# Sparse attention in a two-layer trunk: heads in pairs at the products with the values, the compressed branch padded to 128 rows, output projections in three parts

## The chip, the cores and the metric

The kernel runs on one core of one Trainium2 chip. The metric is the device time of one execution in microseconds (us), lower is better. Every product is made in float32 accuracy by splitting each operand into a high and a low float32r part (named `hi` and `lo`, or `wh` and `wl` for weights) and adding three products: high by high, high by low and low by high.

## The reference, cut to what matters

The program is a decoder trunk of two layers over one sequence of 256 tokens with a model width of 2048. Layer 0 mixes tokens by native sparse attention (NSA) with 16 heads of 128 columns in 4 groups of 4; layer 1 mixes them by gated linear attention (GLA). After each mixer comes an MLP with 8192 hidden columns.

```
o_cmp = einsum(p_cmp, v_cmp)      # 15 compressed keys, padded to 16
o_sel = ...; o_win = ...          # at 256 tokens both are causal attention over all keys
o = gts[...,0:1]*o_cmp + gts[...,1:2]*o_sel + gts[...,2:3]*o_win
y = o.reshape(b, s, nh*d) @ w_out # 2048 x 2048
x = x + y;  x = x + squared_relu_mlp(rms_norm(x))
```

A group of 4 heads shares its keys and values. The gates are multiplied into the probabilities, so that all three branches of a head are summed in one accumulator.

## The kernel before, in words

**The plan.** The program text is written out by a planner, the class `Plan` (line 34). It keeps a clock for each engine; each helper adds its own estimated cost to the clock (`mm` on line 158, `transpose` on 167, `act`, `copy`, `tt`, `ts`). Side work is written as Python generators ("streams"), spawned with `W.spawn`. A stream yields the planned time at which it may go on (`W.ready`: the end of the work that made its inputs, plus `MARGIN` of 250 ns) and the buffers that it needs. `W.tick` is called after every few matmuls of the main work and lets each stream whose time has come emit its next instructions; it returns at once while ACT or DVE is planned to be more than `slack` (2500 ns) behind PE. `W.drain` runs one stream to its end at the place where the main work needs it, whether its inputs are ready on the chip or not. So the costs in `mm` and `transpose` decide where each side instruction lands in each engine's queue, in the whole program. `mode_b`, which the MLP uses for its first product, passes its own slack of 2500 or 5000 ns; `a_half`, which makes all projections, uses the default.

**Main work of the NSA layer.** `nsa` (973) makes ten projections of 512 columns: compressed keys, compressed values, then twice keys, values and the queries of two groups. Each is 16 row tiles x 2 token tiles x 3 products = 96 matmuls of 512 columns, by `mode_a` and `a_half`. Each half unit of weights (512 KB) is split into `wh` by ACT and `wl` by DVE, three half units ahead of use.

**A head.** `queries` (1281) transposes a group's queries, takes an `operand()` tile `oT` for the group's output and spawns `attend` (1305) for each head. `attend` makes scores and exponentials for the two token tiles into one of 3 tiles `p`, applies gates, transposes `p` in six 128x128 pieces, and the compressed probabilities `p3` (high, high and low part, 3 x 16 = 48 columns for each token tile) in two more. The transposes go to two `aux` banks (of 4) in PSUM; ACT copies them to `pT` and `pTc` and DVE makes the low part of `pT`. `pT` has one slot (980), so that a head's transposes are emitted after the products of the head before. Lines 1407 to 1423 make the products with the values: for four blocks of keys three matmuls each, over 256 or 128 tokens, and one with `vC` on 48 rows:

```
mm(dst, v[:, 0, t, gs], ph_, ...)       # n = 256 or 128 columns
mm(dst, v[:, 0, t, gs], pl_, ...)
mm(dst, v[:, 1, t, gs], ph_, ...)
mm(po[:, 0:T], vC[:, g, :], pTc, ...)   # 48 rows, 256 columns
```

**Compressed keys and values.** `compress` (1118) works in four steps with tiles of `qT`, `pT` and `op` slots; for the values it ends with four small products that give `vC` (lines 1248 to 1264). The heads of the first group wait for both compress streams.

**Output projection.** `out_proj` (608), used by NSA and GLA, takes the contraction (16 row tiles, 4 for each group) in two halves of 8 tiles; in each half come the four column blocks `b`, each with 48 matmuls. `add_block` (602) has DVE add the two accumulators to the residual `xt`. In the first block of a half, `ready` (1450) drains the query stream and the head that each tile needs. After the last half's block `b`, `after.start(b)` (732) spawns the next MLP's preparation of that block: 8 transposes on PE, 4 scaled copies on ACT, 4 low parts on DVE, then two squares on ACT. The MLP's first unit (`mode_b`, 584) uses row tiles 0 to 7 of two weight units and then tiles 8 to 15, and drains the preparation of each tile (`prep.before`, 661).

Of the kernel before, what the change touches and what calls it, by code (L numbers as in the profile page):

```python
# [10 lines left out]
F32 = mybir.dt.float32  # L11
# [7 lines left out]
P = 128  # L19
T = 256  # L20
# [13 lines left out]
class Plan:  # L34
# [62 lines left out]

    def tick(self, slack=2500.0):
        taken = set()
        for s in list(self.streams):  # L100
            if max(self.t["act"], self.t["dve"]) > self.t["pe"] + slack:
                return
            if s["ready"] <= self.t["pe"]:
                if not (taken & set(s["need"])) and self.can(s["need"]):
                    self._step(s)
                else:
                    taken |= {tag for tag, n in s["need"].items() if not self.can({tag: n})}
# [16 lines left out]
def trunk_kernel(ctx: ExitStack, tc: tile.TileContext, a: dict, out: bass.AP):  # L124
# [33 lines left out]
    def mm(dst, lhsT, rhs, **kw):  # L158
        n = free(rhs)
        if lhsT.dtype == F32R:  # L160
            c = n / 2.4 + 3 if n >= 128 else 107.0
        else:
            c = max(4 * n / 2.4 + 3, 214.0)
        W.run("pe", c, [dst], [lhsT, rhs])
        nc.tensor.matmul(dst, lhsT, rhs, skip_group_check=True, **kw)  # L165

    def transpose(dst, src, idn):
        W.run("pe", 56.0 if src.dtype == F32R else 110.0, [dst], [src])
        nc.tensor.transpose(dst, src, idn)  # L169
# [331 lines left out]
    for b in range(10):  # L501
        for kg in range(4):
            weights.both(a["nsa_in"][b, kg])
        if b == 3:
            weights.both(a["nsa_gate"], 48)

    def out_units(w):
        for half in range(2):
            for b in range(NB):
                for kg in range(2):  # L510
                    weights.both(w[b, 2 * half + kg])
    out_units(a["nsa_out"])


# [93 lines left out]
    def out_proj(oTs, after, ready):  # L608

        for half in range(2):  # L610
            for b in range(NB):
                ps = acc()
                mode_a(oTs, ps, list(range(8 * half, 8 * half + 8)), ready if b == 0 else None)
                add_block(ps, b)
                if half == 1:
                    after.start(b)
            for g in (2 * half, 2 * half + 1):
                W.give(oTs[g])
# [354 lines left out]
    def nsa(prep, after):  # L973
        op = prep.op
        G, HPG = 4, 4
        with tc.tile_pool(name="nsa1", bufs=1) as s1, tc.tile_pool(name="nsa2", bufs=1) as s2:
            t4 = slotted(s2, "t4", 2)
            qtile = slotted(s2, "qT", 5)
            ptile = slotted(s2, "p", 3)
# [4 lines left out]
            def tables():  # L984
# [21 lines left out]
                nc.sync.dma_start(stack, a["gate_stack"])  # L1006
                vsel = s1.tile([48, 16], F32, name="vsel")[:, 0:2]
                nc.sync.dma_start(vsel, a["cmp_sel"])
                cst.update(identr=identr, maskr=maskr, gcol=gcol, w2=w2, pe=pe, stack=stack, vsel=vsel)
                yield 50000.0  # L1010
                vcopy(maskr, maskf)
                ts(gcol[:, 0:1], gcol[:, 0:1], SCALE, None, ALU.mult)
                W.give(maskf, W.t["dve"])
# [29 lines left out]
            vv = [s1.tile([P, 2, NT, 512], F32R, name=f"vv{i}") for i in range(2)]  # L1043
            vC = s1.tile([48, G, P], F32R, name="vC")
            gt = s1.tile([P, NT, 48], F32, name="gt")
# [72 lines left out]
            def compress(ps, which):  # L1118
# [127 lines left out]
                else:  # L1246

                    ge3 = zpool.tile([P, G, 3, 16], F32, tag="sq", name="ge3", bufs=2)
                    vcopy(ge3, ge.rearrange("p (g c) -> p g c", c=16).unsqueeze(2).to_broadcast([P, G, 3, 16]))
                    yield W.ready(ge3), {"aux": 1, "p": 2}  # L1250
                    pv = aux([P, 512])
                    for g in range(G):
                        mm(pv[:48, g * P:(g + 1) * P], ge3[:, g, :, :].rearrange("p a c -> p (a c)"),
                           w2[:, 1, :], start=True, stop=True)
                    vh = ptile([48, 512], F32R)
                    copy(vh, pv[:48, :])
                    yield W.ready(vh)
                    vl = ptile([48, 512])
                    tt(vl, pv[:48, :], vh.bitcast(F32), ALU.subtract)
                    W.give(pv, W.t["dve"])  # L1260
                    ts(vl, vl, cst["vsel"][:, 1:2], None, ALU.mult)
                    stt(vC.rearrange("p g d -> p (g d)"), vh.bitcast(F32), cst["vsel"][:, 0:1], vl, ALU.mult, ALU.add)
                    W.give(vh, W.t["dve"])
# [17 lines left out]
            def queries(ps, g, heads, waits):  # L1281
                yield 0.0, {"t4": 1}
                qs = t4([P, NT, 512])
                yield from normed(qs, ps)
                yield 0.0, {"rope": 1}
                rope(qs, cst["tabs"][0])
                for w in waits:
                    while not w["done"]:
                        yield 0.0
                yield 0.0, {"op": 1}  # L1290
                oT = operand()
                oTs[g] = oT
                for hh in range(2):
                    yield W.ready(qs), {"aux": 1, "qT": 2}
                    pt = transposed(qs, [(2 * hh + j) * P for j in range(2)])
                    qTs = [qtile([P, 2, T], F32R) for _ in range(2)]
                    yield from evac_splits([(qTs[j][:, 0, :], qTs[j][:, 1, :],
                                             pt[:, j, :, :].rearrange("p t k -> p (t k)"), cst["gcol"][:, 0:1])
                                            for j in range(2)])
                    give(pt)  # L1300
                    for j in range(2):
                        heads.append(W.spawn(attend(g, 2 * hh + j, qTs[j], oT)))
                W.give(qs)

            def attend(g, h, qT, oT):
                k = kT[g]
# [69 lines left out]

                p3 = small.tile([P, NT, 3, 16], F32R, tag="p3", name=nm("p3"))
                copy(p3[:, :, 0:2, :], pc.unsqueeze(2).to_broadcast([P, NT, 2, 16]))
# [3 lines left out]
                tt(p3[:, :, 2, :], pc, p3[:, :, 0, :].bitcast(F32), ALU.subtract)  # L1382
                yield W.ready(p, p3), {"aux": 2, "pT": 1}

                pta = aux([P, 512])
                ptb = aux([P, 512])
                ptc = ptb[:, 256:512].bitcast(F32R)
# [9 lines left out]
                pT = pttile([P, 2, 768], F32R)  # L1397
                pTc = small.tile([48, T], F32R, tag="pTc", name=nm("pTc"), bufs=2)
# [4 lines left out]
                tt(pT[:, 1, 0:512], pta, pT[:, 0, 0:512].bitcast(F32), ALU.subtract)  # L1403
                W.give(pta, W.t["dve"])
                tt(pT[:, 1, 512:768], ptb[:, 0:256], pT[:, 0, 512:768].bitcast(F32), ALU.subtract)
# [12 lines left out]
                mm(po[:, 0:T], vC[:, g, :], pTc, start=False, stop=True)  # L1418
                W.give(pT)
                copy(oT[:, h, 0, :], po[:, 0:T])  # L1420
                yield W.ready(oT)
                tt(oT[:, h, 1, :], po[:, 0:T], oT[:, h, 0, :].bitcast(F32), ALU.subtract)
                W.give(po, W.t["dve"])
# [424 lines left out]
def _constants():  # L1848
# [28 lines left out]
    c["gate_stack"] = np.concatenate([np.eye(48), np.eye(48)], 0).astype(np.float32)  # L1877
    low = (np.arange(48) // 16 == 1).astype(np.float32)
    c["cmp_sel"] = np.stack([1.0 - low, low], 1)

# [85 lines left out]
```

## Time and profile before

| what | value |
|---|---|
| median of 3 runs | 2179.98 us (2179.89 to 2184.03) |
| the profiled execution, its own time | 2175.89 us |
| its span in the profile | 2174.1 us |
| PE (matmul) busy | 2162.6 us, 99% |
| DVE, ACT, POOL busy | 1742.7 us (80%), 1363.7 us (63%), 151.4 us (7%) |
| granted TensorE clock | 1.0 in every slice (its upper level, 2.4 GHz) |
| DMA | 483.81 MB, mean 223 GB/s |

The span runs from the first to the last instruction; some 1.8 us of the execution lie around it. A matmul's own duration in the trace overlaps with that of its neighbours, so what one costs is read from the distance between the starts of two neighbours.

### The profile page before, as it was taken

What the parts mean: (1) busy time and instruction counts of PE and PEld (TensorE: products, weight loads), DVE (VectorE), ACT (ScalarE), POOL (GpSimd) and SP (SyncE); (2) the same over time, 40 slices, a digit from 0 to 9 for tenths busy, and PEclk for the clock granted to TensorE, in tenths of its full rate; (3) what the DMA queues carried; (4) which work ended last, traced back from release to release, by engine and by line L of the source; (5) the groups of instructions that cost most, each with busy time, mean ns of one, the idle gap of its engine ahead of it and who ended that gap; (6) DMA issues with size and microseconds to landing.
All of it is one profiled execution on the core that took longest, in us unless ns stands there. A gap on an engine that the chain in (4) does not pass through costs nothing.

```text
span 2174.1 us, 29700 instructions
## 1 busy us (share of the span) xinstructions
PE 2162.6 (99%) x11131; PEld 1821.0 (84%) x11131; DVE 1742.7 (80%) x2369; ACT 1363.7 (63%) x2118; POOL 151.4 (7%) x189
## 2 busy tenths in 40 slices
PE   9999999999999999999999999999999999999999
PEld 7888888888888888888888888888888888888887
DVE  6687677689999999998666656666899999999985
ACT  6567766566666666666566555445666666667663
POOL 0010000001001001001000000000000010010010
PEclk9999999999999999999999999999999999999999
DMA  7653352669879879888655354456698798798784
GB/s 262 220 194 136 136 184 92 221 229 284 268 247 276 277 237 281 269 254 232 201 193 181 136 174 156 155 185 221 226 290 258 249 275 277 240 280 278 241 233 154
DMA packets 83087, 483.81 MB, mean 223 GB/s; under 512 B 10496, under 2 KB 13200, under 8 KB 35072
## 3 DMA queue, kind: packets, MB, share of 16 engines
q1 hardware_dynamic: 61264, 403.78, 50.6%
q0 software_dynamic: 21680, 78.15, 18.1%
q8 instruction: 87, 1.43, 0.3%
q14 instruction: 56, 0.46, 0.1%
HBM read 405.35 MB, written 2.10 MB: 187 GB/s over the span
## 4 chain that ended last, share of the span: by engine, by line
PE 97%; DMA 2%; DVE 1%; ACT 0%; SPq 0%; issue 0%; POOL 0%; POOLq 0%; ACTq 0%; DVEq 0%
PE psa L165 58%; PE psx L165 37%; PE psx L169 2%; DMA sraw<-sraw 1%; DMA raw<-in_nsa_in_dram 1%; DMA sraw<-in_mlp_down_dram 0%; DVE wl L200 0%; ACT wh L196 0%; DVE att L1693 0%; SPq L1807 0%; DVE pT L200 0%; ACT p L192 0%; SPq L411 0%; ACT pT L196 0%; DVE xt L204 0%
## 5 line engine op out<-in xcount | busy, mean ns | idle before, releaser
L165 PE MATMUL psa<-wh,op 128*128 128x512 f32 x2616 | 861.7, 394 | 1.7 <-ACT wh L196 1.7
L200 DVE TENSOR_TENSOR wl<-raw,wh 128x1024 fp32r<-128x1024 f32 (+1 forms) x529 | 642.6, 1220 | 230.0 <-ACT wh L196 227.6
L196 ACT CAST wh<-raw 128x1024 fp32r<-128x1024 f32 (+1 forms) x533 | 557.7, 1047 | 288.9 <-PE psa L165 241.6
L165 PEld LDWEIGHTS psa<-wh,op 128*128 128x128 f32 x2616 | 491.0, 188 | 106.9 <-ACT wh L196 2.5
L200 DVE TENSOR_TENSOR wl<-sraw,wh 128x1024 fp32r<-128x1024 f32 x392 | 473.5, 1219 | 56.3 <-ACT wh L196 54.4
L165 PE MATMUL psx<-op,wh 128*128 128x512 f32 (+1 forms) x2080 | 515.9, 390 | 0.0
L165 PE MATMUL psa<-wl,op 128*128 128x512 f32 x1308 | 510.8, 391 | 1.9 <-DVE wl L200 1.9
L196 ACT CAST wh<-sraw 128x1024 fp32r<-128x1024 f32 x392 | 409.6, 1049 | 139.4 <-PE psa L165 59.2
L165 PEld LDWEIGHTS psx<-op,wh 128*128 128x128 f32 (+1 forms) x2080 | 384.9, 188 | 78.7
L165 PE MATMUL psa<-wh,ht 128*128 128x512 f32 x1128 | 385.1, 394 | 0.3 <-ACT wh L196 0.3
L165 PEld LDWEIGHTS psx<-op,wl 128*128 128x128 f32 x2048 | 279.5, 190 | 20.0
L165 PEld LDWEIGHTS psa<-wl,op 128*128 128x128 f32 x1308 | 245.9, 188 | 51.3 <-DVE wl L200 4.8
L165 PE MATMUL psx<-op,wl 128*128 128x256 f32 x2048 | 285.9, 282 | 0.0
L165 PEld LDWEIGHTS psa<-wh,ht 128*128 128x128 f32 x1128 | 213.1, 189 | 41.6 <-ACT wh L196 0.7
L165 PE MATMUL psa<-wl,ht 128*128 128x512 f32 x564 | 221.9, 393 | 0.0
L337 POOL DMA_DIRECT2D sraw<-sraw x140 | 120.2, 956 | 1296.3 <-DVE pz L200 430.1
L204 DVE SCALAR_TENSOR_TENSOR xt<-psa,r,xt 128x512 f32<-128x512 f32 x212 | 157.4, 745 | 25.3 <-PE psa L165 24.1
L196 ACT COPY zz<-psx 128x256 f32<-128x256 f32 x128 | 47.7, 372 | 160.8 <-PE psx L165 160.7
L165 PEld LDWEIGHTS psa<-wl,ht 128*128 128x128 f32 x564 | 106.1, 188 | 16.9
L200 DVE TENSOR_TENSOR sraw<-sraw,sraw 128x1024 f32<-128x1024 f32 x84 | 102.6, 1221 | 1.0
L200 DVE TENSOR_TENSOR zz<-psx,zz 128x256 f32<-128x256 f32 x128 | 53.6, 419 | 14.5 <-ACT zz L196 14.5
L196 ACT CAST ht<-pz 128x896 fp32r<-128x896 f32 (+1 forms) x40 | 37.1, 928 | 28.1 <-DVE pz L204 27.3
(195 smaller groups left out, 1205.4 us busy)
## 6 DMA issues: line engine op xcount, KB each, us to landing
raw<-in_mlp_up_dram SPq DMA_DIRECT2D x128, 1024.0 KB, 7.4
sraw<-in_mlp_down_dram SPq DMA_DIRECT2D x112, 1024.0 KB, 11.2
sraw<-sraw POOLq DMA_DIRECT2D x140, 512.0 KB, 9.4
raw<-in_gla_in_dram SPq DMA_DIRECT2D x48, 1024.0 KB, 4.9
raw<-in_nsa_in_dram SPq DMA_DIRECT2D x38, 1024.0 KB, 4.9
raw<-in_nsa_out_dram SPq DMA_DIRECT2D x16, 1024.0 KB, 4.9
raw<-in_mlp_down_dram SPq DMA_DIRECT2D x16, 1024.0 KB, 4.9
raw<-in_gla_out_dram SPq DMA_DIRECT2D x16, 1024.0 KB, 4.9
```

Source lines behind the costliest of these rows:

```text
L165: nc.tensor.matmul(dst, lhsT, rhs, skip_group_check=True, **kw)
L169: nc.tensor.transpose(dst, src, idn)
L196: nc.scalar.copy(dst, src)
L200: nc.vector.tensor_tensor(dst, x, y, op=op)
L204: nc.vector.scalar_tensor_tensor(dst, x, s, y, op0=op0, op1=op1)
L337: nc.gpsimd.dma_start(dst, src, accum_op=ALU.add)
```

## The change: what it does, and the diff

Two heads share one `pT` tile, now with both heads' transposed probabilities, high and low, 1664 columns each; the second head of a pair waits until the first has allocated it, and only the second makes the products, over both heads at once. Their output bank `po` holds 2 x 256 columns, and the ACT copy and the DVE low part serve both heads. `p3` becomes one of three fixed tiles of 2 x 4 x 16 columns, zeroed once, transposed as one 128x128 piece that holds both token tiles; `vC` gets a copy for each token tile with zero rows where the other tile's probabilities lie, so that its product has 128 rows and runs once for each token tile. `qT` has 4 slots instead of 5. `out_proj` and the order of its weight units go over groups 0 and 1, then 2, then 3. In the plan a float32r matmul costs max(n/2.4+13, 109) ns and a transpose 109 ns, and the default slack is 3200.

```diff
-    def tick(self, slack=2500.0):
+    def tick(self, slack=3200.0):
...
-            c = n / 2.4 + 3 if n >= 128 else 107.0
+            c = max(n / 2.4 + 13.0, 109.0)
...
-        W.run("pe", 56.0 if src.dtype == F32R else 110.0, [dst], [src])
+        W.run("pe", 109.0, [dst], [src])
...
+    PARTS = ((0, 1), (2,), (3,))
+
     def out_units(w):
-        for half in range(2):
+        for part in PARTS:
             for b in range(NB):
-                for kg in range(2):
-                    weights.both(w[b, 2 * half + kg])
+                for kg in part:
+                    weights.both(w[b, kg])
...
-        for half in range(2):
+        for part in PARTS:
             for b in range(NB):
                 ps = acc()
-                mode_a(oTs, ps, list(range(8 * half, 8 * half + 8)), ready if b == 0 else None)
+                mode_a(oTs, ps, [4 * g + j for g in part for j in range(4)], ready if b == 0 else None)
                 add_block(ps, b)
-                if half == 1:
+                if part == PARTS[-1]:
                     after.start(b)
...
-            qtile = slotted(s2, "qT", 5)
+            qtile = slotted(s2, "qT", 4)
...
+                for p3 in p3s:
+                    ts(p3.rearrange("p t a c -> p (t a c)"), ident, 0.0, None, ALU.mult)
...
-            vC = s1.tile([48, G, P], F32R, name="vC")
+            vC = s1.tile([P, NT, G, P], F32R, name="vC")
+            p3s = [s1.tile([P, NT, 4, 16], F32R, name=f"p3{i}") for i in range(3)]
...
-                        mm(pv[:48, g * P:(g + 1) * P], ge3[:, g, :, :].rearrange("p a c -> p (a c)"),
+                        mm(pv[:, g * P:(g + 1) * P], ge8[:, g, :, :].rearrange("p a c -> p (a c)"),
...
-                yield W.ready(p, p3), {"aux": 2, "pT": 1}
-
+                second = h % 2
+                if second:
+                    while "pT" not in pair:
+                        yield 0.0
+                yield W.ready(p, p3), {"aux": 2} if second else {"aux": 2, "pT": 1}
+
+                if not second:
+                    pair["pT"] = pttile([P, 2, 1664], F32R)
+                pT = pair["pT"]
...
-                for t in range(NT):
-                    transpose(ptc[:48, t * P:(t + 1) * P], p3[:, t, :, :].rearrange("p a c -> p (a c)"),
-                              cst["identr"])
+                transpose(ptc, p3.rearrange("p t a c -> p (t a c)"), cst["identr"])
...
-                copy(pT[:, 0, 0:512], pta)
-                copy(pT[:, 0, 512:768], ptb[:, 0:256])
-                copy(pTc, ptb[:48, 256:512])
+                copy(pT[:, second, 0:512], pta)
+                copy(pT[:, second, 512:896], ptb[:, 0:384])
...
-                yield W.ready(pT, pTc), {"aux": 1}
-                po = aux([P, 512])
+                if not second:
+                    pair["first"] = True
+                    return
+                while "first" not in pair:
+                    yield 0.0
+                yield W.ready(pT), {"aux": 1}
+                po = aux([P, 2, T])
...
-                    dst = po[:, T - n:T]
-                    ph_, pl_ = pT[:, 0, lo:lo + n], pT[:, 1, lo:lo + n]
+                    dst = po[:, :, T - n:T]
+                    ph_, pl_ = pT[:, :, lo:lo + n], pT[:, :, 896 + lo:896 + lo + n]
...
-                mm(po[:, 0:T], vC[:, g, :], pTc, start=False, stop=True)
+                for t in range(NT):
+                    mm(po[:, :, t * P:(t + 1) * P], vC[:, t, g, :], pT[:, :, 768:896], start=False, stop=(t == 1))
...
-                if not heads[kt // 4][kt % 4]["done"]:
-                    W.drain(heads[kt // 4][kt % 4])
+                if not heads[kt // 4][kt % 4 | 1]["done"]:
+                    W.drain(heads[kt // 4][kt % 4 | 1])
```

## Rows read from the trace of the kernel before

**Rows 1.** The page's first part (busy time of the engines) and its fourth (the chain of work that ended last, share of the span by engine).

```profile
PE 2162.6 (99%) x11131; PEld 1821.0 (84%) x11131; DVE 1742.7 (80%) x2369; ACT 1363.7 (63%) x2118; POOL 151.4 (7%) x189
...
PE 97%; DMA 2%; DVE 1%; ACT 0%; SPq 0%; issue 0%; POOL 0%; POOLq 0%; ACTq 0%; DVEq 0%
```

**Rows 2.** The waits of PE over the whole span: us in total, times, longest.

```profile
PE psa L165 <- ACT wh L196: 2.0, 4, 0.9
PE psa L165 <- DVE wl L200: 1.9, 5, 0.8
PE psx L165 <- DVE pT L200: 1.8, 3, 1.0
```

**Rows 3.** Windows: busy time of each engine over most of the heads' work, up to the second half of the output projection, and over the first block of that half from its fifth row tile on. Columns: stretch, length, then busy us of PE, PEld, DVE, ACT, POOL, granted clock, DMA share, GB/s.

```profile
161.00:348.00 187.00, 187.00 (x1022) 159.61 (x1021) 133.25 (x317) 133.24 (x451) 12.68 (x12) 1.00 0.43 147
...
355.70:373.10 17.40, 15.28 (x101) 12.57 (x99) 10.38 (x30) 10.32 (x41) 0.00 (x0) 1.00 0.18 62
```

**Rows 4.** PE's groups of instructions between 160 and 374 us, shapes apart: count, busy us, mean ns of one, idle before.

```profile
L165 PE MATMUL psx<-pT,vv 128*128 128x256 f32 x96 | 18.0, 292 | 1.7 <-DVE pT L200 1.3 <-ACT pT L196 0.3
...
L165 PE MATMUL psx<-pT,vv 128*128 128x128 f32 x96 | 12.5, 266 | 0.0
...
L165 PE MATMUL psx<-pTc,vC 48*128 48x256 f32 x16 | 6.1, 381 | 0.0
L169 PE MATMUL psx<-identr,p 128*48 128x128 f32 x32 | 5.8, 264 | 0.0
```

**Rows 5.** The chain of work that ended last, in order of time: start us, length us, engine, output, line, count. The first two are transposes and projection matmuls (512 columns), the third is half matmuls of 512 and half of 256 columns (the MLP).

```profile
378.14 0.87 PE psx L169 x8
379.01 10.90 PE psa L165 x48
...
526.61 5.56 PE psx L165 x32
```

**Rows 6.** PE's timeline around the products of one head: start us, length us, instruction, count.

```profile
311.77 1.54 PE L165 MATMUL psx<-pT,vv 128*128 128x256 f32 x12
313.24 0.38 PE L165 MATMUL psx<-pTc,vC 48*128 48x256 f32 x1
313.55 0.50 PE L165 MATMUL psa<-wh,op 128*128 128x512 f32 x1
313.88 0.39 PE L165 MATMUL psa<-wl,op 128*128 128x512 f32 x1
```

**Rows 7.** The same view around the eight transposes of one head.

```profile
337.49 0.82 PE L169 MATMUL psx<-cid,p 128*128 128x128 f32 x6
338.07 0.36 PE L169 MATMUL psx<-identr,p 128*48 128x128 f32 x2
338.27 0.44 PE L165 MATMUL psa<-wh,op 128*128 128x512 f32 x1
338.55 0.40 PE L165 MATMUL psa<-wl,op 128*128 128x512 f32 x1
```

**Rows 8.** The same view at the end of the compressed values.

```profile
154.86 1.07 PE L165 MATMUL psx<-w,ge 128*48 128x128 f32 x8
155.86 0.50 PE L165 MATMUL psa<-wh,op 128*128 128x512 f32 x1
```

**Rows 9.** The same view where the second half of the output projection drains the heads of group 3; in brackets the idle time before and what ended it.

```profile
359.07 0.62 PE L165 MATMUL psx<-kT,qT 128*128 128x256 f32 x3
360.14 0.52 PE L165 MATMUL psx<-kT,qT 128*128 128x272 f32 x2 [0.45 <-DVE pT L200]
...
366.24 0.30 PE L165 MATMUL psx<-pT,vv 128*128 128x256 f32 x1
367.53 1.52 PE L165 MATMUL psx<-pT,vv 128*128 128x256 f32 x11 [0.99 <-DVE pT L200]
...
369.92 0.36 PE L169 MATMUL psx<-identr,p 128*48 128x128 f32 x2
370.62 0.38 PE L165 MATMUL psx<-pT,vv 128*128 128x256 f32 x1 [0.34 <-ACT pT L196]
371.34 1.52 PE L165 MATMUL psx<-pT,vv 128*128 128x256 f32 x11 [0.34 <-DVE pT L200]
```

**Rows 10.** PE's groups between 349.0 and 411.2 us (as in rows 4): the matmuls with the high part of the weights in the second half of the output projection; those with the low part are half as many.

```profile
L165 PE MATMUL psa<-wh,op 128*128 128x512 f32 x128 | 41.3, 394 | 0.0
```

**Rows 11.** PE's timeline at the products of the last head of group 2.

```profile
342.64 1.54 PE L165 MATMUL psx<-pT,vv 128*128 128x256 f32 x12
```

**Rows 12.** Windows (as in rows 3) over one block of the last half of the output projection, in NSA and in GLA.

```profile
387.70:399.47 11.77, 11.77 (x57) 9.84 (x56) 7.76 (x11) 6.99 (x12) 0.00 (x0) 1.00 0.54 182
1465.10:1476.87 11.77, 11.77 (x57) 9.83 (x57) 7.76 (x10) 6.98 (x14) 0.00 (x0) 1.00 0.52 180
```

**Rows 13.** The timelines of DVE and PE at the start of the first MLP.

```profile
417.85 0.87 DVE L204 SCALAR_TENSOR_TENSOR op<-psx,cid,op 128x256 fp32r<-128x256 f32 x2
...
417.69 2.00 PE L165 MATMUL psx<-op,wh 128*128 128x512 f32 x8
```

**Rows 14.** The page's fifth part, the low part of the weights and the hand-over of the MLP's first product: busy us, mean ns, idle before.

```profile
L200 DVE TENSOR_TENSOR wl<-sraw,wh 128x1024 fp32r<-128x1024 f32 x392 | 473.5, 1219 | 56.3 <-ACT wh L196 54.4
...
L200 DVE TENSOR_TENSOR zz<-psx,zz 128x256 f32<-128x256 f32 x128 | 53.6, 419 | 14.5 <-ACT zz L196 14.5
```

**Rows 15.** PE's timeline in GLA, matmuls of 64 columns whose moving operand is read in strided pieces.

```profile
1190.62 1.39 PE L165 MATMUL psx<-g 128*32 128x64 f32 x32
```

More of the change, by code (lines that the diff above doesn't have):

```diff
@@ L608, in out_proj @@
     def out_proj(oTs, after, ready):
-        for half in range(2):
+        for part in PARTS:
             for b in range(NB):
                 ps = acc()
-                mode_a(oTs, ps, list(range(8 * half, 8 * half + 8)), ready if b == 0 else None)
+                mode_a(oTs, ps, [4 * g + j for g in part for j in range(4)], ready if b == 0 else None)
                 add_block(ps, b)
-                if half == 1:
+                if part == PARTS[-1]:
                     after.start(b)
-            for g in (2 * half, 2 * half + 1):
+            for g in part:
                 W.give(oTs[g])
@@ L1006, in tables @@
                 nc.sync.dma_start(stack, a["gate_stack"])
-                vsel = s1.tile([48, 16], F32, name="vsel")[:, 0:2]
+                vsel = s1.tile([P, 32], F32, name="vsel")[:, 0:4]
                 nc.sync.dma_start(vsel, a["cmp_sel"])
@@ L1246, in compress @@
                 else:
-                    ge3 = zpool.tile([P, G, 3, 16], F32, tag="sq", name="ge3", bufs=2)
-                    vcopy(ge3, ge.rearrange("p (g c) -> p g c", c=16).unsqueeze(2).to_broadcast([P, G, 3, 16]))
-                    yield W.ready(ge3), {"aux": 1, "p": 2}
+                    yield W.ready(ge), {"aux": 1, "p": 3}
+                    ge8 = ptile([P, G, 8, 16])
+                    vcopy(ge8, ge.rearrange("p (g c) -> p g c", c=16).unsqueeze(2).to_broadcast([P, G, 8, 16]))
+                    yield W.ready(ge8), {"p": 2}
                     pv = aux([P, 512])
                     for g in range(G):
-                        mm(pv[:48, g * P:(g + 1) * P], ge3[:, g, :, :].rearrange("p a c -> p (a c)"),
+                        mm(pv[:, g * P:(g + 1) * P], ge8[:, g, :, :].rearrange("p a c -> p (a c)"),
                            w2[:, 1, :], start=True, stop=True)
-                    vh = ptile([48, 512], F32R)
-                    copy(vh, pv[:48, :])
+                    W.give(ge8)
+                    vh = ptile([P, 512], F32R)
+                    copy(vh, pv)
                     yield W.ready(vh)
-                    vl = ptile([48, 512])
-                    tt(vl, pv[:48, :], vh.bitcast(F32), ALU.subtract)
+                    vl = ptile([P, 512])
+                    tt(vl, pv, vh.bitcast(F32), ALU.subtract)
                     W.give(pv, W.t["dve"])
-                    ts(vl, vl, cst["vsel"][:, 1:2], None, ALU.mult)
-                    stt(vC.rearrange("p g d -> p (g d)"), vh.bitcast(F32), cst["vsel"][:, 0:1], vl, ALU.mult, ALU.add)
+                    for t in range(NT):
+                        vt = vC[:, t, :, :].rearrange("p g d -> p (g d)")
+                        ts(vt, vl, cst["vsel"][:, 2 * t + 1:2 * t + 2], None, ALU.mult)
+                        stt(vt, vh.bitcast(F32), cst["vsel"][:, 2 * t:2 * t + 1], vt.bitcast(F32), ALU.mult, ALU.add)
                     W.give(vh, W.t["dve"])
@@ L1300, in queries, with attend @@
                     give(pt)
+                    pair = {}
                     for j in range(2):
-                        heads.append(W.spawn(attend(g, 2 * hh + j, qTs[j], oT)))
+                        heads.append(W.spawn(attend(g, 2 * hh + j, qTs[j], oT, pair)))
                 W.give(qs)
-            def attend(g, h, qT, oT):
+            def attend(g, h, qT, oT, pair):
                 k = kT[g]
@@ L1375, in attend @@
                     act(pv0, pv0, AF.Copy, scale=wg[:, 1 + b:2 + b])
-                p3 = small.tile([P, NT, 3, 16], F32R, tag="p3", name=nm("p3"))
+                p3 = p3s.pop(0)
                 copy(p3[:, :, 0:2, :], pc.unsqueeze(2).to_broadcast([P, NT, 2, 16]))
@@ L1382, in attend @@
                 tt(p3[:, :, 2, :], pc, p3[:, :, 0, :].bitcast(F32), ALU.subtract)
-                yield W.ready(p, p3), {"aux": 2, "pT": 1}
+                second = h % 2
[6 more added lines that the diff above has]
+                pT = pair["pT"]
                 pta = aux([P, 512])
                 ptb = aux([P, 512])
-                ptc = ptb[:, 256:512].bitcast(F32R)
+                ptc = ptb[:, 256:384].bitcast(F32R)
                 for b in range(2):
@@ L1392, in attend @@
                     transpose(ptb[:, b * P:(b + 1) * P], p[:, 544 + b * P:544 + (b + 1) * P], ident)
-                for t in range(NT):
-                    transpose(ptc[:48, t * P:(t + 1) * P], p3[:, t, :, :].rearrange("p a c -> p (a c)"),
-                              cst["identr"])
+                transpose(ptc, p3.rearrange("p t a c -> p (t a c)"), cst["identr"])
+                p3s.append(p3)
                 W.give(p)
-                pT = pttile([P, 2, 768], F32R)
-                pTc = small.tile([48, T], F32R, tag="pTc", name=nm("pTc"), bufs=2)
-                copy(pT[:, 0, 0:512], pta)
-                copy(pT[:, 0, 512:768], ptb[:, 0:256])
-                copy(pTc, ptb[:48, 256:512])
+                copy(pT[:, second, 0:512], pta)
+                copy(pT[:, second, 512:896], ptb[:, 0:384])
                 yield W.ready(pT)
-                tt(pT[:, 1, 0:512], pta, pT[:, 0, 0:512].bitcast(F32), ALU.subtract)
+                tt(pT[:, second, 896:1408], pta, pT[:, second, 0:512].bitcast(F32), ALU.subtract)
                 W.give(pta, W.t["dve"])
-                tt(pT[:, 1, 512:768], ptb[:, 0:256], pT[:, 0, 512:768].bitcast(F32), ALU.subtract)
+                tt(pT[:, second, 1408:1664], ptb[:, 0:256], pT[:, second, 512:768].bitcast(F32), ALU.subtract)
                 W.give(ptb, W.t["dve"])
-                yield W.ready(pT, pTc), {"aux": 1}
-                po = aux([P, 512])
+                if not second:
[5 more added lines that the diff above has]
+                po = aux([P, 2, T])
                 v = vv[g // 2]
@@ L1417, in attend @@
                     mm(dst, v[:, 1, t, gs], ph_, start=False, stop=False)
-                mm(po[:, 0:T], vC[:, g, :], pTc, start=False, stop=True)
+                for t in range(NT):
+                    mm(po[:, :, t * P:(t + 1) * P], vC[:, t, g, :], pT[:, :, 768:896], start=False, stop=(t == 1))
                 W.give(pT)
-                copy(oT[:, h, 0, :], po[:, 0:T])
+                copy(oT[:, h - 1:h + 1, 0, :], po)
                 yield W.ready(oT)
-                tt(oT[:, h, 1, :], po[:, 0:T], oT[:, h, 0, :].bitcast(F32), ALU.subtract)
+                tt(oT[:, h - 1:h + 1, 1, :], po, oT[:, h - 1:h + 1, 0, :].bitcast(F32), ALU.subtract)
                 W.give(po, W.t["dve"])
@@ L1877, in _constants @@
     c["gate_stack"] = np.concatenate([np.eye(48), np.eye(48)], 0).astype(np.float32)
-    low = (np.arange(48) // 16 == 1).astype(np.float32)
-    c["cmp_sel"] = np.stack([1.0 - low, low], 1)
+    rows = np.arange(P) // 16
+    c["cmp_sel"] = np.stack([np.isin(rows, r) for t in (0, 4) for r in ((t, t + 2), (t + 1,))], 1).astype(np.float32)
     cum = np.zeros((P, 2, 8, P), np.float32)
```

## The prediction

> **What bounds the kernel now.** I read the shares first: the matmul engine is busy 99% of the span, and the chain that ended last is PE for 97% [rows 1]. Busy matmuls overlap, so the second view is what PE waited for: three lines of about 2 us each in 2174 [rows 2]. PE's instruction stream itself is the bound, and DVE and ACT count only where PE waits for them. The windows say where that is in the attention: from 161 to 348 us PE has no idle time at all, with DVE and ACT busy 71% of it (133.25 and 133.24 of 187.00); from 355.7 to 373.1 us it idles 17.40 - 15.28 = 2.12 us [rows 3]. So each distance between starts of matmuls that the change shortens before 348 us is gained in full, and in the drain there are two us of waiting to win as well. The granted clock is 1.00 in both stretches [rows 3], which is the upper level, 2.4 GHz; I expect it to stay there.
>
> **Prices of a matmul.** 48 matmuls of 512 columns take 10.90 us, so one takes 0.227. 16 of 512 and 16 of 256 columns take 5.56 us; the pair takes 0.3475 and one of 256 columns 0.120. Eight 128-column transposes take 0.87 us, 0.109 each [rows 5].
>
> **The products with the values.** Before, each of 16 heads makes six matmuls of 256 columns, six of 128 and one on 48 rows: 96, 96 and 16 in all [rows 4]. From the first start to the next other matmul is 313.55 - 311.77 = 1.78 us, and that next matmul of 512 columns takes 313.88 - 313.55 = 0.33 instead of 0.227, so a head costs 1.78 to 1.89 us [rows 6]. After, a pair makes six matmuls of 512 and six of 256 columns, and two of 256 on 128 rows for the compressed branch: 6 x 0.227 + 8 x 0.120 = 2.33 us. The columns streamed are the same 5120 for a pair; gone are the matmuls of 128 columns, which cost nearly as much as 256, and the one on 48 rows: 0.31 us against 0.120, with 313.24 - 311.77 = 1.47 us for the twelve before it, and 0.10 more in its follower [rows 6]. Saved: 16 x 1.78 (or 1.89) - 8 x 2.33 = 9.9 to 11.6 us. I take 11.4, since most products are followed by a 512-column matmul as in these rows.
>
> The gain from padding rests on a row: a 48-row matmul is dearer than a 128-row one and slows its neighbours [rows 6]. The Trainium skill (TensorEngine Tiling (Array Packing), Key Properties) says that a change of tiling mode drains the engine, and the trace agrees with it: 0.31 us against 0.120. The Trainium skill's other page (TensorE: Matmul & The Clock Gate, Part 2, step 1) says that the number of rows doesn't matter for a weight load; by that alone the padding would bring nothing, and the sum would be 16 x 0.3, some 5 us, smaller. The row decides for the first.
>
> **Transposes.** Eight for a head cost 338.27 - 337.49 = 0.78 us and 338.55 - 338.27 - 0.227 = 0.05 in the follower [rows 7]; seven of 128 columns cost 7 x 0.109 = 0.76. Saved 16 x 0.07 = 1.1 us.
>
> **End of the compressed values.** Eight records take 155.86 - 154.86 = 1.00 us [rows 8]; at 128 columns 8 x 0.109 = 0.87. Saved 0.1 us.
>
> **The drain.** In the old second half, 24 matmuls after its start, the last four heads are run to their end [rows 9, 10]. Beyond the price of their matmuls PE stands still 1.07 - 0.36 = 0.71, then 1.29 - 0.12 = 1.17, 0.70 - 0.20 = 0.50 and 0.72 - 0.12 = 0.60 us [rows 9], 3.0 in all; by busy time it is 2.12 [rows 3]. After, group 3 is first read in the last part, behind four blocks of 24 matmuls of part two, 96 x 0.227 = 21.8 us, instead of 24 x 0.227 = 5.4. That is 16.3 us more room for work that took 17.4 us in the drain, nearly all of it PE's own. I take 2.8 us as gained.
>
> What is late next is group 2, needed where part two starts. Its last products began at 342.64 us [rows 11], the half began at about 348.6 (the first 24 matmuls of 0.227 end at the drain, 355.7, with other work between). That is 6 us of room, and the pair's last products need both heads. The shared `pT` frees once for two heads, so transposes need not wait for each head's products, which speaks for an earlier end. If it is late, PE waits as in rows 9, about 0.7 to 1.2 us for each hand-over: 0 to 3 us. I take 0.5, near zero, since the windows before show no wait [rows 3].
>
> **The last part and the start of the MLPs.** A block of the last part has 24 matmuls and 8 transposes of the MLP's preparation: 5.45 + 0.87 = 6.32 us instead of 11.77. In that time DVE must do half the weights of before, but as many additions and low parts: its 7.76 us less two weight splits of 1.22 is 5.3 us [rows 12, 14]; ACT has less to do still (6.99 us before its weights are halved). Both fit, DVE at 84%, so no queue builds up, in NSA or GLA. Four more blocks bring eight additions, all on DVE, at no cost while that holds. But the preparation of block 2 now ends 5.45 us later against the MLP's start. Before, block 3's last low part ended at 417.85 + 0.87 = 418.72 us and its reader, the seventh matmul of a run from 417.69, came at 419.05 [rows 13]: a margin of 0.33 us. Block 2's four low parts take 2 x 0.87 = 1.74 us in that queue, partly done by then. So each MLP start loses 0 to 1.4 us; I take 0.4, twice 0.4 = 0.8.
>
> **Edits at nothing.** The slot less of `qT`, the zeroing of `p3s`, two more DVE steps for `vC` (under 2 us) and a first wait for three `p` tiles lie on streams while PE is full, 161 to 348 us [rows 3]; without that cover they would cost their own length, 2 to 3 us. DMA count and bytes stay: only the order of the out units on SP's queue changes. ACT loses the `pTc` copy of each head. The wait of the second head stops no engine: a stream that waits emits nothing.
>
> **New costs in the plan, and the slack.** The plan priced a 512-column matmul at 512/2.4 + 3 = 216 ns; now it is 226, and the row says 227 [rows 5]. PE was 5% slower than planned, which gave side work a cushion; this cushion goes, in all layers. The plan prices the low part of a half unit at 1024 x 1.042 + 75 = 1142 ns, the row 1219 [rows 14]; 77 ns is inside the 250 ns of `MARGIN`. So I put it at 0, with ends from 1 us won (deeper slack, earlier heads) to what the third rival costs.
>
> **Sum.** 11.4 + 1.1 + 0.1 + 2.8 = 15.4 us gained, 0.5 + 0.8 = 1.3 lost: 14.1 us. The profiled execution took 2175.89 us (span 2174.1 and 1.8 around it), so 2161.8. The median of the runs stands 4.1 us above it: 2165.9, forecast as 2166. Its own range: least 9.9 + 1.1 + 2.1 - 3 - 2.8 = 7.3, most 11.6 + 1.1 + 0.1 + 3.0 + 1 = 16.8 us, so 2163 to 2173.
>
> **Rivals.**
>
> First, strided outputs. Eight of a pair's 14 matmuls write two runs of 128 columns with a gap, and all read two runs. No row shows a strided write. For reading, 32 matmuls of 64 columns in strided pieces take 1.39 us, 0.04 each [rows 15], no sign of a price. If each of the eight took twice its time, 8 x 8 x 0.120 = 7.7 us would go: 2173.6. The Trainium skill (PSUM — Partial Sum Buffer, Specifications) says that any non-contiguous access pattern slows matmuls significantly; rows 15 don't show that for reads. Chance 6%.
>
> Second, the waits move. If the pairs are late at both new starts (groups 2 and 3, two pairs each), with 2 us of ACT and DVE hand-over laid open for a pair, 8 us go and the drain's 2.8 are won all the same: 2173.4. For it speaks that the pair's products wait for the later head; against it the 16 us of room. Chance 8%.
>
> Third, and slower: the plan's cushion. If emitted consumers reach PE before ACT and DVE are done, each hand-over stalls. There are 128 from the MLP's first product alone [rows 14]; at 0.15 us each (twice the 77 ns) that is 19 us, and the total 2166 + 19 = 2185. It decides from the point where the lag of a hand-over exceeds the margin of 250 ns. At half that price the gain is eaten up, 2176. For it: rows 14's 7% over the plan and no cushion. Against it: three waits of 2 us now [rows 2]. Chance 8%, split evenly between slower and no difference.
>
> That the change doesn't do what it says has little room: the matmul counts follow from the loops.
>
> **How the numbers follow.** The forecast has 78%; faster by over 0.2% (4.4 us, about what a measurement of this kernel can tell from no change) holds in it and in both first rivals but for their late ends: 0.88. Within 0.2%: half of the third and a mix of the first two, 0.07. Slower: 0.05. The range takes the forecast's own, the first two rivals, and some of the 4 us by which the runs differ among themselves: 2158 to 2176.
>
> **What would show it.** Of the products: 48 + 64 records in place of 208 (96, 96 and 16), 2.3 us from the first of a pair to the next other matmul, no 48-row record. Of transposes: 7 records in 0.76 us. Of the drain: no PE wait for `pT` around the new last part. Of the MLP starts: any gap in the first 32 matmuls, ended by DVE `op`. I am wrong if the strided matmuls lie more than 0.125 us apart, if PE waits for `pT` before part two, or if PE's waits in the MLPs grow.

## The result, and the profile after

The changed kernel took 2158.14 us (median of 4 runs, 2156.62 to 2158.59) beside 2180.12 us for the kernel before (4 runs, 2179.89 to 2184.03): ratio 0.9895, 95% interval [0.988, 0.991]. It is faster, as forecast, but by 22 us where 14.1 were worked out, so that the time lies at the lower edge of the range of 2158 to 2176 us and below the sum's own 2163 to 2173. The profiled execution took 2158.59 us, its span 2156.8. Two executions of the study stand far above all others and are left out of every comparison: one of the kernel before (2364.19 us, at a granted clock of 0.85) and one of the variant without padding (5527.3 us).

The page after, first and fourth part, answers to [rows 1]; the waits of PE over the span answer to [rows 2].

```profile
PE 2144.7 (99%) x11019; PEld 1810.5 (84%) x11019; DVE 1750.9 (81%) x2382; ACT 1358.2 (63%) x2094; POOL 155.4 (7%) x189
...
PE 92%; DMA 5%; DVE 1%; ACT 1%; issue 0%; SPq 0%; POOL 0%; POOLq 0%; DVEq 0%; ACTq 0%
```

```profile
PE psa L165 <- DVE wl L200: 2.8, 7, 0.8
PE psa L165 <- ACT wh L196: 2.5, 5, 1.1
...
PE psx L165 <- DVE qT L200: 0.8, 1, 0.8
```

PE is still the bound, with 112 matmuls fewer. The line for `pT` is gone from the waits; a single wait for `qT` is new. The windows of [rows 3], over the same stretches, show that PE has no idle time left in either of them:

```profile
161.00:348.00 187.00, 187.00 (x997) 159.67 (x996) 145.13 (x347) 141.05 (x478) 13.59 (x12) 1.00 0.43 149
355.70:373.10 17.40, 17.40 (x86) 14.56 (x84) 13.03 (x17) 7.32 (x9) 0.00 (x0) 1.00 0.50 165
```

PE's timeline has a pair's products (against [rows 6]), one head's transposes (against [rows 7]) and the blocks of the last part with the MLP's first matmuls (against [rows 5, 13]):

```profile
296.49 0.82 PE L169 MATMUL psx<-cid,p 128*128 128x128 f32 x6
297.06 0.30 PE L169 MATMUL psx<-identr,p 128*128 128x128 f32 x1
297.20 0.46 PE L165 MATMUL psx<-kT,qT 128*128 128x272 f32 x2
...
302.51 2.28 PE L165 MATMUL psx<-pT,vv 128*128 128x512 f32 x12
304.62 0.40 PE L165 MATMUL psx<-pT,vC 128*128 128x256 f32 x2
304.86 0.77 PE L165 MATMUL psx<-kT,qT 128*128 128x256 f32 x5
...
379.91 1.03 PE L169 MATMUL psx<-cid,xt 128*128 128x128 f32 x8
386.24 1.03 PE L169 MATMUL psx<-cid,xt 128*128 128x128 f32 x8
392.58 1.03 PE L169 MATMUL psx<-cid,xt 128*128 128x128 f32 x8
...
396.64 0.39 PE L165 MATMUL psa<-wh,op 128*128 128x512 f32 x1
396.86 1.98 PE L165 MATMUL psx<-op,wh 128*128 128x512 f32 x8
398.68 0.64 PE L165 MATMUL psx<-op,wl 128*128 128x256 f32 x4
```

A pair takes 304.86 - 302.51 = 2.35 us, seven transposes 297.20 - 296.49 = 0.71, a block of the last part 386.24 - 379.91 = 6.33. The first matmul of MLP 0 starts at 396.86 us; before it was 411.25. That is 14.4 us, almost what the sum said. The other 7 to 8 us between the medians come later. I compared the start of every projection and MLP matmul (9744, in the same order in both kernels). The lead grows evenly by 0.3 to 0.4 us for each 78 us in both MLPs, some 3 us in each, and by 0.2 us in GLA; on top of that come single steps where one of the two executions waits for weights. In these two executions the steps take back some 3 us, so that the lead ends at 17.3 us. No line of the change touches the MLP.

### The profile page after: what moved, and what is told of

It reads as the page before. It is cut to its first block, busy times and chain, and to the rows that moved or that the text cites. A ratio compares the mean times of both kernels' runs of the same rounds, so it can differ in the third digit from the quotient of the medians.

```text
span 2156.8 us, 29488 instructions
## 1 busy us (share of the span) xinstructions
PE 2144.7 (99%) x11019; PEld 1810.5 (84%) x11019; DVE 1750.9 (81%) x2382; ACT 1358.2 (63%) x2094; POOL 155.4 (7%) x189
## 4 chain that ended last, share of the span: by engine, by line
PE 92%; DMA 5%; DVE 1%; ACT 1%; issue 0%; SPq 0%; POOL 0%; POOLq 0%; DVEq 0%; ACTq 0%
PE psa L165 56%; PE psx L165 35%; DMA sraw<-sraw 3%; PE psx L169 2%; DMA sraw<-in_mlp_down_dram 1%; DMA raw<-in_nsa_in_dram 1%; ACT wh L196 1%; DVE wl L200 1%; DVE att L1715 0%; SPq L1829 0%; POOL sraw L337 0%; DVE kT L204 0%; DVE qT L200 0%; SPq L419 0%; SPq L411 0%
```

## The experiments

**How the first execution of before fell, and whether the change's trace repeats.** The kernel before and the changed kernel, each unchanged, profiled again.

> The kernel before, unchanged, on one chip with the next three runs. Its first profiled execution took 2175.89 us, its timed runs a median of 2180.12, and the prediction carried that distance of 4.1 us over to the changed kernel. Theory A: the 4 us are a stall inside some executions of the kernel before, not of the chip; then this run's executions spread from about 2176 to 2184, and where this profile is longer than the first one the whole difference lies at one or two places of PE's stream. Theory B: the 4 us are the chip's, all stages in proportion; then each stage of this profile is longer or shorter by the same share (0.2%) than in the first one.

Measured: 2179.62 us (2176.59 to 2181.41, 11 runs), ratio 0.9993 [0.9984, 1.0002]; the profiled execution took 2179.62. Its trace follows the first one up to MLP 0 (which starts at 411.14 us); the difference between the two comes in single steps where the MLPs wait for weights. Over the study, 69 runs of the kernel before have a median of 2179.7 us and one of them is below 2176, so the profiled execution of 2175.89 was among the shortest.

> The changed kernel, unchanged, on the chip of the other three. Theory A: its executions lie within 2 us of 2158, and the gain over the kernel before is 17 us against the shortest executions of before and 22 against the usual ones. Theory B: the gain against this chip's own runs of before is 14.4 (the time at which the first MLP starts earlier in the two first profiles) to 17.3 us.

Measured: 2158.23 us (2156.02 to 2159.84, 4 runs), ratio 0.9894 [0.9881, 0.9907]. MLP 0 starts at 395.85 us. The growing lead in the MLPs is there again, so it is no accident of one execution, and the gain against the usual executions of before is again 22 us.

**The plan alone, and the parts alone**, each in the kernel before:

```diff
-    def tick(self, slack=2500.0):
+    def tick(self, slack=3200.0):
-            c = n / 2.4 + 3 if n >= 128 else 107.0
+            c = max(n / 2.4 + 13.0, 109.0)
-        W.run("pe", 56.0 if src.dtype == F32R else 110.0, [dst], [src])
+        W.run("pe", 109.0, [dst], [src])
```

> The kernel before with the plan's edits alone: matmul and transpose costs, default slack 3200. By the prediction 0 us, with ends of 1 us won and 19 lost; PE's work is the same, so only waits can move: the 2.1 to 3.0 us of waiting in the drain of group 3, and the first 25 us. Rival (the plan's cushion): each of 128 hand-overs of the MLP stalls 0.1 us or more, 2190 us and PE waits in both MLPs. A further theory: if the extra gain beyond the forecast comes from the plan, this run gains 4 to 8 us.

Measured: 2179.75 us, ratio 0.9995 [0.9986, 1.0005]. MLP 0 starts at 410.15 us, 1.0 earlier. By itself the plan is worth nothing that can be told.

```diff
-        for half in range(2):
+        for part in ((0, 1), (2,), (3,)):
```

> The kernel before with the output projections in parts of 8, 4 and 4 row tiles alone. By the prediction the drain's 2.8 us are gained and 0.8 us lost at the two MLP starts, 0 to 0.5 at part two: about 2 us faster than before. Rival (late pairs or heads): a wait of 2 us or more for pT at the start of part two or three, so no gain. PE's products and transposes as before.

Measured: 2178.07 us, ratio 0.9988 [0.998, 0.9997]; MLP 0 starts at 407.81 us, 3.3 earlier, and PE waits for nothing between 20 and 430 us. The 2 us by the medians are what was expected.

**What the MLPs gain.** In the changed kernel `p3` and `pTc` have left the pool `small` (3 x 384 and 2 x 1024 bytes of a partition) and `ge3` has left `zpool` (2 x 256). The pools lie one behind the other, so all tiles of the MLP's own pool (`ht`, `zz`, `sraw`, `pz`) moved down by 3712 bytes; the weights' tiles `wh`, `wl` and `op` did not move. The next two kernels change that alone, with the same instructions in the same order on every engine: the kernel before with the three tiles put in the attention's pool, and the changed kernel with an unused tile of 3712 bytes more in front.

```diff
-                p3 = small.tile([P, NT, 3, 16], F32R, tag="p3", name=nm("p3"))
+                p3 = s2.tile([P, NT, 3, 16], F32R, tag="p3", name=nm("p3"), bufs=3)
-                pTc = small.tile([48, T], F32R, tag="pTc", name=nm("pTc"), bufs=2)
+                pTc = s2.tile([48, T], F32R, tag="pTc", name=nm("pTc"), bufs=2)
...
-            zp.tile([P, 32], F32, tag="pad", name=nm("pad"))
+            zp.tile([P, 32 + 928], F32, tag="pad", name=nm("pad"))
```

> The kernel before with the same instructions in the same order on every engine; only the tiles p3, pTc and ge3 lie in the attention's own pool instead of the long-lived small pools, so that the MLP's pool (ht, zz, sraw, pz) begins 3712 bytes lower, as it does in the changed kernel. Theory C (the gain beyond the forecast is where the MLP's tiles lie in the memory): matmuls with ht as stationary operand lie about 227 instead of 233 ns apart where two high ones follow each other, about 6 us in both MLPs together, so some 2174 us. Theory D (the extra is less waiting for weights in the MLPs, or chance): as the kernel before, 2180 us, and the distances stay at 233.

> The changed kernel with the same instructions; the pad at the start of the MLP's pool is 3712 bytes longer, so that the MLP's tiles lie where they lay in the kernel before. Theory C: the 6 us are lost again, 2164 us, and the distance of two high matmuls with ht is 233 ns. Theory D: 2158 us and 227 ns, as the changed kernel.

Measured: before with its tiles moved down 2175.7 us, ratio 0.9983 [0.9974, 0.9992]; the changed kernel with them moved back 2163.76 us (2160.21 to 2164.7), ratio 0.9928 [0.9916, 0.994], against 0.9894 and 0.9895 without. The attention doesn't change by it (MLP 0 starts at 411.15 and at 395.77). The place of the tiles is worth some 3.5 to 6 us by the medians, both ways.

**Which places.** Three pads more, of 128, 256 and 384 bytes, in the changed kernel (`32 + 32`, `32 + 64`, `32 + 96` in the line above).

> The changed kernel, same instructions on every engine in the same order; only the unused pad ahead of the MLP's tiles is 128 bytes longer, so that each of them (ht, zz, sraw, pz) lies 128 bytes higher in a partition: ht begins at 142208, which leaves 384 when divided by 512, as in the kernel before (145792); in the changed kernel 142080 leaves 256. Theory M (what counts is where a tile lies within 512 bytes): the distance between starts of high-by-high pairs of the MLP's second product goes back to 233.2 ns from 227.3, the sum over all MLP pairs rises by about 5.3 us, and the kernel takes 2163.6 us. Theory N (what counts is the address as a whole, or the distance to other tiles 3712 bytes away): 128 bytes do nothing, 227.3 ns and 2158.2 us.

> The same with a pad 256 bytes longer than in the changed kernel: ht begins at 142336, a multiple of 512, as the weights' tiles do. Theory M leaves open which places within 512 bytes are good: if only the one seen with 227.3 ns (256 left over) is, 233.2 ns and 2163.6 us; if every multiple of 256 is good, 227.3 ns and 2158.2 us; if a multiple of 512 is better still, below 227 ns and below 2157 us. Theory N: 2158.2 us.

> The same with a pad 384 bytes longer: ht begins at 142464, which leaves 128 when divided by 512. Theory M: dear like the other odd multiple of 128, 233.2 ns and 2163.6 us, if it is the multiple of 256 that counts. Theory N: 227.3 ns and 2158.2 us.

Measured: 2165.12 us for 128 bytes (0.9928 [0.9916, 0.994]), 2159.11 for 256 (0.9901 [0.9887, 0.9914]) and 2164.18 for 384 (0.9925 [0.991, 0.9939]). What counts is where the tiles lie: at multiples of 256 bytes it is cheap, at odd multiples of 128 it is dear; multiples of 512 are no better than of 256. The chain of work that ended last, in order of time, of the first two of these kernels in the same stretch of MLP 0 (start us, length us, what, matmuls); first 128 bytes, then 256:

```profile
510.29 2.77 PE psa L165 x12
513.06 5.56 PE psx L165 x32
518.62 2.77 PE psa L165 x12
...
568.49 5.53 PE psa L165 x24
```

```profile
509.49 2.75 PE psa L165 x12
512.24 5.56 PE psx L165 x32
517.80 2.75 PE psa L165 x12
...
567.49 5.47 PE psa L165 x24
```

The product into `psx` takes the same; the second product of the MLP, into `psa`, is shorter by 0.02 us in twelve matmuls, 0.06 in 24. Single distances show more. In the second product a matmul of the low part of `ht` by `wh` is followed by one of a high part of `ht` by `wh`. From the first to the second it is 233.2 ns (mean of 367) in both traces of before and with the pads of 3712, 128 and 384 bytes, and 227.3 ns in the changed kernel, in the shifted kernel before and with 256. The other neighbours change by less than 2 ns.

Taken matmul by matmul, in the same order, the distances in the two MLPs differ between a dear and a cheap kernel by 5.9 to 6.1 us in all five pairs of traces that I compared (the first traces of before and after, the second ones, before with the shifted kernel before, the pad of 3712 bytes with the changed kernel, the pad of 128 with that of 256). Single differences of more than 30 ns, which are waits, are left out of this; GLA differs by 0.2 us or less.

**Two parts instead of three**, in the changed kernel:

```diff
-    PARTS = ((0, 1), (2,), (3,))
+    PARTS = ((0, 1), (2, 3))
```

> The changed kernel with the output projections in two halves of 8 tiles as before. By the prediction's step on the drain: PE waits for pT again in the second half's first block, 2 to 3 us, 0.8 us less at the MLP starts: about 2160 us. Rival: pairs shorten the chain of the heads so far that the drain has no wait even with halves; then 2157 to 2158.

Measured: 2164.3 us (2161.86 to 2165.83), ratio 0.9932 [0.9919, 0.9944], some 6 us dearer by the medians (8 by the ratios), three times what was expected. MLP 0 starts at 399.16 us, 2.3 later. PE's timeline shows the last pair run to its end in the second half:

```profile
356.93 0.50 PE L165 MATMUL psx<-pT,vv 128*128 128x512 f32 x1 [0.40 <-ACT pT L196]
357.65 2.13 PE L165 MATMUL psx<-pT,vv 128*128 128x512 f32 x11 [0.23 <-DVE pT L200]
359.62 0.39 PE L165 MATMUL psx<-pT,vC 128*128 128x256 f32 x2
360.70 0.50 PE L165 MATMUL psa<-wh,op 128*128 128x512 f32 x1 [0.68 <-ACT op L196]
```

The waits shown are 1.3 of the 2.3 us. Another 0.8 us is a wait for `wl` at 996 us, still in MLP 0, that the changed kernel doesn't have. The rest, 1.6 us by the two spans and 3 by the medians, lies in waits for weights in the MLPs, which differ from one execution to the next; they are not told apart.

**Pairs without the padding.** The changed kernel with the compressed branch on 48 rows (`p3`, `pTc`, `ge3` and `vC` as in the kernel before, `pTc` for two heads).

> The changed kernel without the padding: vC and the compressed probabilities on 48 rows, one product of 512 columns for a pair, two transposes for a head instead of one. By the prediction's price for 48 rows (0.31 against 0.12 us for 256 columns, 0.09 in the matmul before and 0.10 in the one behind) a pair's products cost 0.38 us more, 3.0 us in eight, and transposes 0.07 us for a head, 1.1 us: 4 us more, and by theory C the MLP's pool lies 2560 bytes lower than in the kernel before instead of 3712, which no run here prices. Rival (rows don't matter): the products cost the same or less, since two matmuls of 256 columns become one of 512.

The profiled run is the one of 5527.3 us, so its trace can't be compared. Measured from the other five: 2169.4 us, ratio 0.9952 [0.9938, 0.9965]. The expectation was wrong on the addresses: the MLP's tiles lie where they lay in the kernel before, so that the comparison is with the changed kernel whose tiles were moved back, 0.9928. The padding is worth 0.0024, some 5 us, where about 4 were expected; the intervals just overlap, and without a trace the 5 us can't be split into products and transposes.

**The old plan in the changed kernel** (the diff of the plan, undone).

> The changed kernel with the plan of before: matmuls at n/2.4+3, transposes at 56 or 110 ns, slack 2500. The MLP's tiles lie where they lie in the changed kernel. The plan alone was worth 0 in the kernel before (0.9995). Theory P (the plan is worth nothing here either): 2158 us, within 2. Rival (with pairs, side work is emitted too early under the old costs, and PE meets pT or oT before they are done): PE waits for pT in the attention or for op in the MLPs, 1 to 4 us, 2159 to 2162 us, and the attention's end moves by as much.

Measured: 2166.11 us (2163.46 to 2167.35), ratio 0.993 [0.9918, 0.9942]: 7 to 8 us dearer (the smaller figure against the pad of 256 bytes, measured beside it), and MLP 0 starts at 401.96 us, 5.1 later. The expectations were 0, or 1 to 4 us. The 1200th projection matmul starts at 346.5 us, against 354.7 under the new plan. As 0.8 us of this is the wait for `qT`, which the old plan doesn't have, PE has been given some 7 us less of the heads' work by then, and the last pair comes up unfinished when the last part drains it. PE's waits between 20 and 425 us, then its timeline:

```profile
PE psx L169 <- DVE p L200: 1.2, 1, 1.2
PE psx L169 <- ACT p L192: 1.1, 1, 1.1
PE psa L165 <- ACT op L196: 0.7, 1, 0.7
PE psa L165 <- DVE wl L200: 0.6, 1, 0.6
PE psx L165 <- ACT pT L196: 0.4, 1, 0.4
PE psx L165 <- DVE pT L200: 0.2, 1, 0.2
```

```profile
371.92 0.33 PE L169 MATMUL psx<-cid,p 128*128 128x128 f32 x1 [1.13 <-ACT p L192]
373.50 0.76 PE L169 MATMUL psx<-cid,p 128*128 128x128 f32 x5 [1.25 <-DVE p L200]
...
375.45 3.48 PE L165 MATMUL psx<-pT,vv 128*128 128x512 f32 x11 [0.16 <-DVE pT L200]
378.76 0.40 PE L165 MATMUL psx<-pT,vC 128*128 128x256 f32 x2
```

The last group took 378.76 - 375.45 = 3.31 us; the same eleven matmuls took 359.62 - 357.65 = 1.97 in the trace above. The windows (columns as in [rows 3]) show what lies between:

```profile
366.00:370.00 4.00, 4.00 (x19) 3.25 (x19) 3.90 (x10) 1.17 (x2) 0.00 (x0) 1.00 0.67 201
370.00:372.00 2.00, 0.87 (x9) 0.68 (x7) 2.00 (x4) 1.40 (x4) 0.00 (x0) 1.00 0.29 123
372.00:374.00 2.00, 0.75 (x6) 0.56 (x7) 1.54 (x4) 0.29 (x2) 0.00 (x0) 1.00 0.49 111
374.00:376.00 2.00, 1.44 (x6) 0.82 (x5) 1.02 (x2) 0.97 (x2) 0.00 (x0) 0.76 0.96 406
376.00:378.00 2.00, 2.00 (x9) 1.86 (x8) 0.00 (x0) 0.00 (x0) 0.00 (x0) 0.50 0.02 8
```

PE was busy 0.87 + 0.75 of four us, and behind that the granted clock was 0.76 and then 0.50, the lower level of 1.2 GHz. The wait was paid twice: once as idle time, and again in the matmuls behind it.

## Why the prediction was right or wrong

**The attention: right in the sum, 14.4 us against 14.1 (15.3 in the second pair of traces).** To compare by parts I sum the distances from start to next start for each kind of matmul up to the MLP.

- Products with the values: 30.45 to 18.78 us. The old figure holds 0.99 + 0.34 us of waits [rows 9], so the products themselves gave 10.3. The 16 matmuls right behind them gave some 1.5 more (one of 512 columns there took 0.33 us and takes 0.23 now): 11.8 against 11.4. The matmul on 48 rows took 0.31 us in each of the 16 heads; its successor on 128 rows takes 0.118. So the price that the padding rested on was right, and the run without padding gives some 5 us back.
- A pair costs 2.35 us, 2.33 was the forecast, so the first rival has fallen: the eight matmuls of 256 columns that write two runs lie 0.117 to 0.118 us apart. Those of 512 columns, which only read two runs, lie 0.236 apart and not 0.227; why is open.
- Transposes: 13.17 to 11.42, of which 0.34 is the wait that ends at 370.62 us [rows 9], so 1.4 against 1.1, since seven take 0.71 us and not 0.76. Compressed values: 1.00 to 0.81 us, 0.2 against 0.1.
- The drain: its idle 2.12 us [rows 3] are 0; 2.8 were counted. The waits for `pT` are gone.
- Part two and the MLP starts, where 0.5 + 0.8 us were to be lost: nothing is. There is no wait at part two, and at the start of MLP 0 DVE is done with block 2's low parts at 395.74 us, before the first matmul at 396.86. What I had not counted stands in their place: 0.8 us of waiting at 128 us for `qT`, in the compressed branch. The plan alone brings the same wait to the kernel before (0.9 us). That the two nearly cancel is luck.

The gains come to 15.5 us, less 0.8 for `qT` 14.7; what is left to 14.4 and 15.3 lies in waits of the first 25 us, which differ from one execution to the next.

**The failed step: "Edits at nothing".** The edits of the tiles were priced only by their instructions. That `p3`, `pTc` and `ge3` leave their pools also moves every tile of the MLP's own pool, from 384 past a multiple of 512 bytes to 256, and that is 6 us by distances, 3.5 to 6 by the runs. The step put at nothing what the runs show to be a quarter of the gain. With the tiles put back on an odd multiple of 128 bytes the changed kernel takes 2163.76, 2165.12 or 2164.18 us, where 2166 was forecast and 2163 to 2173 was its own range. So the rest of the sum held, and it was right to count from the median of before and not from its short profiled execution. Of the whole 22 us, 14.3 to 15.4 are the attention (from either trace of before to either of after), 6 the place of the tiles, and the last 0.6 to 1.7 us are not told apart from the scatter of the MLPs' waits.

**A second step was wrong, and the result hid it: "New costs in the plan" at 0, with up to 1 us won.** In the kernel before that was so (0.9995). In the changed kernel the plan carries 5.1 of the attention's 14.4 us. The gain in the drain, which I counted as due to the parts, is had by the parts alone in the kernel before (3.3 us, no wait left); with pairs, whose products wait for the later head, it is had only because the new plan brings some 7 us more of the heads' work in ahead of it. With pairs and the old plan the second rival's picture appears, the last pair late at a new start, with 2.3 us of waiting for `p` and a fall of the clock on top. My third rival had the sign of the plan wrong: its fear was that hand-overs come too early, and the runs showed heads that come too late. PE's waits for weights hardly grew (2.8 + 2.5 us over the span, against 1.9 + 2.0 [rows 2] and 2.5 + 1.8 in the second trace of before), where 19 us would have been lost.

## What to carry to other kernels

Where a change frees or takes room in a pool, work out where the tiles of all later stages come to lie, and try a pad: here 128 bytes were worth 6 us of a stage that the change doesn't touch. A planner's costs can't be judged in the kernel before a change: undo them inside the changed kernel, because each part can be worth nothing alone and several us together. Where the main engine is full, a late drain costs its wait and, as under the old plan here, a slower clock behind it.

## What the runs showed of the hardware

Two neighbouring matmuls of 512 columns, both with `wh` and `ht`, start 233.2 ns or 227.3 ns apart, by whether the tiles of the MLP's pool lie at odd multiples of 128 bytes in the partition or at multiples of 256. Why is open: the moved tiles are `ht`, which the matmul reads, but also `zz`, `sraw` and `pz`, which ACT and DVE and the transfers use beside it, and no run moved one of them alone. The place of the matmul's own operands can't be all of it: in more than a third of these products an `op` tile stands in for `ht`. There neither `op` nor `wh` has moved, and yet such neighbours lie 231 ns apart (median) in the dear kernels and 226 to 227 in the cheap ones. In GLA they lie 227 apart in both.

Between 20 us and the last 3 us of the span the clock fell in one place of one of the thirteen traces that record it, behind four us in which PE was busy 1.62; in the drain of the kernel before, with 15.28 busy of 17.40 us [rows 3], it stayed at 1.00.
